# Expert blocks of 32 slots in four column groups, with conditional further blocks, one scatter for four experts and two more ring places

## The chip, the cores and the metric

The kernel runs on one core of a Trainium2 chip. The time is that of one execution on the device, in microseconds. Three executions of the kernel before gave 1189.7, 1192.71 and 1199.96 us; their median, 1192.71 us, is the figure to compare with. About 1% is what a measurement of this kernel can tell from no change.

A core has TensorE (PE; its weight loads are listed apart as PEld), VectorE (DVE), ScalarE (ACT), GpSimd (POOL) and SyncE (SP), which here issues the transfers of the weights. Every engine has an instruction stream of its own, and all five take each branch of the program by themselves.

## What is computed

One layer of a streaming encoder on 256 tokens of 1024 channels: token mixing (state space and latent attention), then 32 experts of which each token uses four. The change lies in the experts alone:

```python
logits = (h @ w_router).astype(jnp.float32) + b_router.astype(jnp.float32)
top_vals, top_idx = lax.top_k(logits, TOP_K)          # TOP_K = 4, N_EXPERTS = 32
gates = jax.nn.softmax(top_vals, axis=-1)
...
gu = xb @ w_gate_up[e] + b_gate_up[e]                 # 1024 x 2048 of each expert
glu = jnp.minimum(gu[:, :D_FF_EXPERT], SWIGLU_LIMIT)
lin = jnp.clip(gu[:, D_FF_EXPERT:], -SWIGLU_LIMIT, SWIGLU_LIMIT)
act = glu * jax.nn.sigmoid(SWIGLU_ALPHA * glu) * (lin + 1.0)
y = act @ w_down[e] + b_down[e]                       # 1024 x 1024 of each expert
return y * g[:, None].astype(y.dtype)
```

Weights and activations are float32. All 32 experts have at least three tokens, so every expert's 12 MB of weights are read once. Counted with the reference's own inputs, the experts 0 to 31 have 28, 70, 19, 8, 59, 32, 20, 24, 3, 26, 28, 53, 43, 14, 61, 29, 30, 27, 34, 51, 25, 9, 32, 35, 58, 20, 24, 37, 32, 31, 43 and 19 tokens: eleven have more than 32, and one, expert 1, more than 64.

## The kernel before

**Loads.** An expert's weights come in 12 loads of 1 MB: eight `gu` (128 rows of the first matrix) and four `dn` (256 rows of the second). `Stream` (line 72 on) keeps the list of loads in order and a list of free buffers; a load goes out on SP's queue as soon as a buffer is free, and `done` gives a buffer back. `RING` (line 69) is 7; buffers of the token mixing join the ring when they fall free, so that in the expert stage there are 18 places.

**One expert** is computed for `CAP` = 64 slots. `gather(e + 1)` (L1170) picks the next expert's tokens by a matmul with one-hots, `gathered` turns them (L1178, four transposes) and scales them into `xT`. `up` (L1191) multiplies `xT` with the first matrix: 32 matmuls of 64 weight columns and 512 streamed columns, two of which run beside each other in the two column halves of the array (the trace lists each float32 matmul as two). `up_out` copies the two banks out (`gs`, ACT L1196 and DVE L1197), `act` turns them with eight transposes (L1207) and applies bias, limits and the sigmoid on DVE and ACT. `down` (L1235) multiplies `ac` with the second matrix: 16 matmuls of 64 by 512. Each second expert, `scatter` (L1270) brings two experts' rows back to their tokens with a gated one-hot (`spread_cols`, `spread_mats` L1259) and DVE adds them to `acc` (L1271).

**Order on TensorE.** TensorE's instructions stand in the order in which the code is written. `down(e - 1)` stands in the middle of `up(e)`, so that the chain from `up` to `ac` on ACT and DVE (copy, transposes, activation) is covered by the first matmuls of the next expert.

**More than 64 tokens.** `overflow` (L1348 to L1362) reads the expert's count into a register of every engine and jumps over its body if the count is at most 64. The body takes further blocks of `OV` = 32 slots in four column groups: gather (L1292), `guo` (L1315), transposes (L1321), activation (L1326 to L1331), `pyo` (L1341), scatter. Short matmuls that nobody reads (`warm`, L1276) stand in the waits of the body. For odd experts the first block is outside of the loop. The jump stands after `up`, only for experts 0, 2, 3 and 31 after the first quarter of it. The places of an expert's `gu` loads are given back after that body (`done` in the loop over the experts).

**The end.** The last expert's second product comes in three parts (`pyl`, L1501), each followed by its scatter (`fin`, L1475), the square sums of the norm and the output.

Of the kernel before, what the change touches and what calls it, by code (L numbers as in the profile page):

```python
# [9 lines left out]
F32 = mybir.dt.float32  # L10
# [34 lines left out]
def constants():  # L45
    """Tables that depend on shapes alone, one row per partition."""
# [18 lines left out]
# rows of the tile of parameters that are turned into columns  # L65
# [41 lines left out]
def body(ctx, tc, a, out, ne=NE):  # L107
# [98 lines left out]
    def ld_nat(k0):  # L206
        """Columns of dt, q_a, k_rope, kv_a."""
# [53 lines left out]
    def ld_last(k):  # L261
        """Four slices of a half of the columns, the second half after the first and by its own halves."""
# [54 lines left out]
    def rstd_of(ss, n, width, name, r=None):  # L317
        """1 / sqrt(ss / width + eps)"""
# [7 lines left out]
    # ================================ token mixing ============================================  # L326
    with ExitStack() as fc:
# [6 lines left out]
        def two(shape, name):  # L334
            """One of two buffers in turn."""
# [14 lines left out]
        def transpose_rows(src, nk, evac_fn, tag, first=0):  # L350
            """evac_fn(k0, n, bank): src[p, t, k*128:...]^T, two k a bank."""
# [9 lines left out]
        # c -> silu, 32 equal columns for each slice of d  # L361
# [40 lines left out]
        # x normalised, transposed  # L402
# [12 lines left out]
        def split(w, th, tl_, n=2048, eng=V, parts=1, heng=A):  # L415
            """Two float32r parts that add up to w."""
# [11 lines left out]
        def mm3(o, x2_, w2, start, stop, **kw):  # L428
            """o += (x0 + x1)(w0 + w1) without x1 w1"""
# [4 lines left out]
        # shift and scale of the first norm, a quarter of d at a time: the tensor engine adds up the  # L434
        # partitions, which leaves columns
# [86 lines left out]
        # parameters by column  # L522
# [17 lines left out]
        # The tensor engine's work from here to the output projection is issued in the order in which it is written.  # L540
        # Attention and the state space run beside each other, the other modulation rows between them.
# [11 lines left out]
        # the gate of the state space  # L553
# [19 lines left out]
        def rope(dst, src, t, n, cos, sin):  # L573
            """dst, src [P, n, 32] of token tile t"""
# [35 lines left out]
        # the other modulation rows: of a group of four 512 wide, on partitions 0, 32, 64, 96  # L610
# [6 lines left out]
        def weighed(k):  # L617
            """The first of the two groups: the slices of d are added up before the tensor engine adds up the partitions."""
# [33 lines left out]
        # convolution over tokens, channels on the partitions  # L652
# [12 lines left out]
        # softplus: max(v, 0) + log1p(exp(-|v|)), log1p(e) = 2 atanh(e / (2 + e))  # L665
# [534 lines left out]
    def act(e, gs, parts=1):  # L1200
# [16 lines left out]
        for i in range(parts):  # L1217
# [6 lines left out]
            if i + 1 < parts:  # L1224
                biased(i + 1)
# [323 lines left out]
```

## Time and profile before

| what | value |
|---|---|
| three executions | 1189.7, 1192.71, 1199.96 us (median 1192.71) |
| the profiled execution | span 1197.9 us |
| TensorE busy | 1081.8 us, 90% of the span |
| DVE, ACT, POOL busy | 38%, 16%, 6% |
| bytes moved | 449.52 MB, 375 GB/s over the span |
| queue of the weights | its packets take 93.1% of 16 DMA engines' span |

The span of the profiled execution is 5.2 us over the median. The token mixing fills the first 190 us; the experts run from 192 us to 1160 us, and the end of the last expert and the output take the rest. In the views, a row of TensorE that begins with 128*64 128x512 is a matmul of 128 rows, 64 weight columns and 512 streamed columns; 128*32 has 32 weight columns. What stands in brackets or behind a bar is the idle time of the engine just before the row and what ended it. "PEq L1349" as a releaser is TensorE's own sequencer at the branch of `overflow`.

### The profile page before, as it was taken

The numbers are of one execution on the slowest core, as the hardware profiler recorded it, in microseconds if no ns is written. First come the engines' busy times: TensorE is split into PE (matmuls) and PEld (weight loads), VectorE is DVE, ScalarE is ACT, GpSimd is POOL, SyncE is SP. The second block draws the span as 40 slices with busy tenths as digits, with TensorE's granted clock in tenths as the row PEclk, the third lists the DMA queues.
The fourth block names the chain that finished last, engine by engine and source line by source line (L and its number), as shares of the span: only waits on it lengthen the run. The fifth ranks groups of instructions, "written<-read, shape, count | busy, mean of one in ns | idle before, by whom it ended". The sixth has DMA issues, their size and how long they took to land. (4 is left out here: it accounts for less than half of the span.)

```text
span 1197.9 us, 13360 instructions
## 1 busy us (share of the span) xinstructions
PE 1081.8 (90%) x5082; PEld 458.4 (38%) x5082; DVE 449.7 (38%) x921; ACT 190.5 (16%) x364; POOL 67.9 (6%) x68
## 2 busy tenths in 40 slices
PE   4999998988998999999989998979898999998887
PEld 3876673333333333333323332323332233333233
DVE  7968744333232323232323232323232133323123
ACT  5375441110000001000000000000000000000003
POOL 1265330000000000000000000000000000000000
PEclk9899998999999999999989998989998889999899
DMA  9969798689989999999999999999999999999980
GB/s 326 337 227 375 262 371 327 275 331 396 389 343 409 416 410 416 417 416 416 417 416 416 416 417 416 417 416 415 395 416 417 417 365 380 416 417 415 416 314 36
DMA packets 95982, 449.52 MB, mean 375 GB/s; under 512 B 10306, under 2 KB 23343, under 8 KB 61011
## 3 DMA queue, kind: packets, MB, share of 16 engines
q1 hardware_dynamic: 95410, 447.43, 93.1%
q8 instruction: 92, 1.51, 0.5%
q14 instruction: 64, 0.52, 0.1%
q10 hardware_dynamic: 416, 0.07, 0.0%
HBM read 446.42 MB, written 1.05 MB: 374 GB/s over the span
## 5 line engine op out<-in xcount | busy, mean ns | idle before, releaser
L1191 PE MATMUL gu<-gu,xT 128*64 128x512 f32 x2048 | 473.7, 610 | 11.7 <-DMA gu<-in_w_gate_up 8.5
L1191 PEld LDWEIGHTS gu<-gu,xT 128*64 128x64 f32 x2048 | 145.9, 140 | 291.3 <-issue 271.9
L1235 PE MATMUL py<-dn,ac 128*64 128x512 f32 x992 | 221.9, 600 | 5.7 <-DVE ac L1223 4.3
L1235 PEld LDWEIGHTS py<-dn,ac 128*64 128x64 f32 x992 | 72.7, 139 | 150.2 <-issue 133.0
L1244 DVE COPY cm<-py 64x512 f32<-64x512 f32 x30 | 20.8, 694 | 214.4 <-ACT cm L1243 214.4
L1270 PE MATMUL pc<-cm,gtm 128*128 128x512 f32 x120 | 70.3, 721 | 16.1 <-PEq L1349 9.0
L1197 DVE COPY gs<-gu 128x512 f32<-128x512 f32 x31 | 21.4, 691 | 168.1 <-PE gu L1191 168.1
L1271 DVE TENSOR_TENSOR acc<-acc,pc 128x512 f32<-128x512 f32 x68 | 46.6, 687 | 73.7 <-PE pc L1270 73.6
L1207 PE MATMUL tp<-ident,gs 128*128 128x128 f32 x256 | 39.1, 298 | 38.3 <-PEq L1349 29.6
L1196 ACT COPY gs<-gu 128x512 f32<-128x512 f32 x32 | 18.7, 585 | 318.2 <-PE gu L1191 318.2
L1170 PE MATMUL pg<-x,oh 128*64 128x512 f32 x256 | 62.7, 608 | 4.1 <-PEq L1349 3.6
L1214 DVE TENSOR_TENSOR u<-tp,biasT 128x512 f32<-128x512 f32 x64 | 42.1, 686 | 50.9 <-PE tp L1207 38.6
L1180 DVE TENSOR_TENSOR xT<-pgt,md 128x512 f32<-128x512 f32 x32 | 22.1, 692 | 90.7 <-PE pgt L1178 90.7
L1207 PEld LDWEIGHTS tp<-ident,gs 128*128 128x128 f32 x256 | 31.8, 152 | 62.5 <-issue 55.8
L1512 POOL TENSOR_TENSOR x<-x,acc 128x512 f32<-128x512 f32 x1 | 1.3, 1262 | 957.6 <-ACT acc L1511 957.6
L1243 ACT COPY cm<-py 64x512 f32<-64x512 f32 x30 | 17.4, 579 | 195.3 <-PE py L1235 195.3
L1270 PEld LDWEIGHTS pc<-cm,gtm 128*128 128x128 f32 x120 | 23.1, 221 | 62.1 <-issue 30.5
L1220 ACT ACTIVATE sg<-u 128x512 f32<-128x512 f32 (+1 forms) x33 | 20.4, 618 | 129.7 <-DVE u L1219 129.7
L1166 DVE TENSOR_SCALAR oh<-cst,rkp,r 128x64 f32<-128x64 f32 x64 | 17.1, 311 | 59.2 <-PE pg L1170 59.2
L1172 ACT COPY xg<-pg 128x512 f32<-128x512 f32 x32 | 18.7, 585 | 111.0 <-PE pg L1170 111.0
L1170 PEld LDWEIGHTS pg<-x,oh 128*64 128x64 f32 x256 | 18.8, 139 | 41.4 <-issue 40.5
L1251 DVE TENSOR_SCALAR go<-cst,rkp,gate 128x64 f32<-128x64 f32 x128 | 30.1, 308 | 0.7 <-DVEq L1349 0.6
(401 smaller groups left out, 964.2 us busy)
## 6 DMA issues: line engine op xcount, KB each, us to landing
gu<-in_w_gate_up SPq DMA_DIRECT2D x256, 1024.0 KB, 17.7
dn<-in_w_down SPq DMA_DIRECT2D x126, 1024.0 KB, 19.9
ada<-in_w_ada SPq DMA_DIRECT2D x16, 1024.0 KB, 5.0
mod<-in_w_ada SPq DMA_DIRECT2D x16, 512.0 KB, 9.5
xbc<-in_w_in SPq DMA_DIRECT2D x4, 1024.0 KB
wo<-in_w_out SPq DMA_DIRECT2D x4, 1024.0 KB
z<-in_w_in SPq DMA_DIRECT2D x2, 1024.0 KB, 5.5
nat<-in_w_in SPq DMA_DIRECT2D x4, 392.0 KB
```

The lines of the kernel that those rows point to most:

```text
L1170: T.matmul(pg[64 * h : 64 * h + 64, :], oh[:, t, :], x[:, t, h * 512 : h * 512 + 512], start=t == 0, stop=t == TT - 1)
L1180: V.tensor_tensor(xT.rearrange("p (h q) s -> p q h s", h=2), pg, a2.rearrange("p (h q) -> p q h", h=2)[:, :, :, None].to_broadcast([P, 4, ...
L1191: T.matmul(gu[h][64 * g : 64 * g + 64, :], xT[:, k, :], ws[k][:, g * 1024 + h * 512 : g * 1024 + h * 512 + 512], start=k == 0, stop=k == K ...
L1197: copy(gs[1], gu[1])
L1207: T.transpose(tp[f // 4][:, f % 4].rearrange("p g s -> p (g s)"), gs[f // 4][:, f % 4 * P : (f % 4 + 1) * P], ident)
L1214: V.tensor_tensor(u[:, hs], tp[h], bv[:, hs, :, None].to_broadcast([P, 4, 2, CAP]), op=OP.add)
L1220: A.activation(sg[:, fs], u[:, fs, 0, :], AF.Sigmoid, scale=1.702)
L1235: T.matmul(py[64 * g : 64 * g + 64, :], ac[:, f, :], wd(f, ch), start=f == 0, stop=f == FT - 1)
L1244: V.tensor_copy(comb[(e & 1) ^ 1][64:128, :], py[64:128, :])
L1251: V.tensor_scalar(go[:, t, j, :], iota, rkp[:, t, ee : ee + 1], gate[:, t, ee : ee + 1], op0=OP.is_equal, op1=OP.mult)
L1270: T.matmul(pc, lhs(t, ch), rhs(ch), start=bias is None, stop=True)
L1271: V.tensor_tensor(acc[:, t, ch * 512 : ch * 512 + 512], acc[:, t, ch * 512 : ch * 512 + 512], pc, op=OP.add)
```

## The change

- **Slots.** The first block of an expert is 32 slots instead of 64. `up` takes the four quarters of the 2048 columns into four column groups of one bank: 32 matmuls of 32 by 512, four beside each other. There is one bank to copy (`gs`, by ACT alone) and four transposes instead of eight.
- **Second product.** `down` takes four quarters of 256 columns into four column groups, turned by `e % 4`, so that four experts fill the 128 rows of two banks: 32 matmuls of 32 by 256. It stands right behind `act` of the same expert; the next expert's `up` follows it.
- **Scatter.** Once for four experts: 8 matmuls of 128 by 256 instead of 4 of 128 by 512 for each two.
- **Further blocks.** `more_up` stands ahead of every expert's `up`: if the count is over 32 it computes slots 32 to 63 from the same `xT` (up, one-hots, activation, into `ovs`), and inside of that, if the count is over 64, a loop over further blocks from a gather of their own. `more_down` stands between `act` and `down` and finishes the second block with `ov_down` (product, copy, scatter). `warm` isn't called there any more.
- **Ring.** `RING` is 9, so 20 places in the expert stage; smaller tiles and a smaller scratch size pay for it. The `gu` places are given back after each of the main `up`'s quarters, the `dn` places within `down`.

The core of the diff:

```diff
-RING = 7
+RING = 9
...
+    def up(xT, ws, s0=0, ks=range(KT), gu=None):
+        if gu is None:
+            gu = mp.tile([P, 512], F32, tag="gu", name="gu", bufs=2)
         for k in ks:
-            for h in range(2):
-                for g in range(2):
-                    T.matmul(gu[h][64 * g : 64 * g + 64, :], xT[:, k, :], ws[k][:, g * 1024 + h * 512 : g * 1024 + h * 512 + 512],
-                             start=k == 0, stop=k == KT - 1)
+            for j in range(4):
+                T.matmul(gu[OV * j : OV * j + OV, :], xT[:, k, s0 : s0 + OV], ws[k][:, j * 512 : j * 512 + 512], start=k == 0, stop=k == KT - 1)
+        return gu
...
+    def down(e, ac, wd, release):
+        i = e % 4
...
         for f in range(FT):
-            for g in range(2):
-                ch = g ^ swap
-                T.matmul(py[64 * g : 64 * g + 64, :], ac[:, f, :], wd(f, ch),
-                         start=f == 0, stop=f == FT - 1)
-        return py
+            for q in range(4):
+                o = OV * ((q + i) % 4)
+                T.matmul(group["py"][q // 2][o : o + OV, q % 2, :], ac[:, f % 4, f // 4, :], wd(f, q * 256, 256), start=f == 0, stop=f == FT - 1,
+                         skip_group_check=True)
+            release(f)
...
+    def more_up(e, n, xT, wg, wd):
+        with tc.If(n > OV):
+            with tc.If(n > CAP):
+                rk = tl([P, TT], "rk")
+                V.tensor_scalar(rk, rkp[:, :, e], float(CAP), None, op0=OP.subtract)
+                with tc.For_i(0, (n - CAP + OV - 1) // OV, 1):
+                    xo = ov_gather(rk)
+                    ov_mats(e, iota[:, :OV], lambda t: rk[:, t : t + 1])
+                    ov_act(e, up(xo, wg))
+                    ov_down(wd)
                     V.tensor_scalar(rk, rk, float(OV), None, op0=OP.subtract)
-
-            if first == CAP:
-                blocks()
-            else:
-                with tc.If(n > first):
-                    blocks()
-                V.tensor_scalar(rk, rkp[:, :, e], float(CAP), None, op0=OP.subtract)
-                ov_down(wd, ov_up(e, rk, wg, tag))
+            gu = up(xT, wg, OV)
+            ov_mats(e, iota[:, OV : 2 * OV], lambda t: rkp[:, t, e : e + 1])
+            ov_act(e, gu)
+            if e == ne - 1:
+                ov_down(wd)
+
+    def more_down(n, wd):
+        with tc.If(n > OV):
+            ov_down(wd)
...
     for e in range(ne):
         wg = [st_.take(f"gu{e}_{k}") for k in range(KT)]
-        wdp, wd = wd, weights_down(e)
-        ahead = e in (0, 2, 3, last)
...
+        wd = weights_down(e)
+        n = nc.values_load(cnt[0:1, e : e + 1], min_val=0, max_val=S)
+        more_up(e, n, xT, wg, wd)
...
+        gu = some_up(range(0, 2))
         if e < last:
             xg = gather(e + 1)
...
+        act(e, turned(gs), ub, sg, ac)
+        if e < last:
+            more_down(n, wd)
+            down(e, ac, wd, lambda f: st_.done(f"dn{e}_{f - 1}") if f % 2 else None)
+            xT = xTn
```

How this stands on TensorE, before: the piece from the last three loads of one expert's `down` (L1235) through the next expert's `up` (L1191) to the branch of `overflow` (L1348, L1349). x4 is the number of matmuls of the row.

```order
L1235 MATMUL py<-dn_2_3625,ac 64x512 x4
L1235 MATMUL py<-dn_4_3627,ac 64x512 x4
L1235 MATMUL py<-dn_6_3629,ac 64x512 x4
L1191 MATMUL gu<-gu_2_3715,xT 64x512 x4
L1191 MATMUL gu<-gu_3_3717,xT 64x512 x4
L1178 MATMUL pgt<-ident,xg 128x128 x4
L1191 MATMUL gu<-gu_4_3719,xT 64x512 x4
L1191 MATMUL gu<-gu_5_3721,xT 64x512 x4
L1191 MATMUL gu<-gu_6_4089,xT 64x512 x4
L1191 MATMUL gu<-gu_7_4091,xT 64x512 x4
L1348 TENSOR_LOAD cnt
L1349 COMPARE_AND_BRANCH
```

The same place after the change: from `more_down` (L1324, L1330) through `down` (L1222) of one expert to the two branches ahead of the next expert's `up` (L1334 is the one on 32, L1335 the one on 64).

```order
L1196 MATMUL tp<-ident,gs 128x128 x4
L1351 COMPARE_AND_BRANCH
L1324 MATMUL pyo<-dn_0_1509,ovs 32x512 x4
L1330 MATMUL pc<-yo,gb 128x512 x4
L1351 UNCONDITIONAL_BRANCH x2
L1222 MATMUL py<-dn_0_1509,ac 32x256 x8
L1222 MATMUL py<-dn_2_1587,ac 32x256 x8
L1222 MATMUL py<-dn_4_1589,ac 32x256 x8
L1222 MATMUL py<-dn_6_1591,ac 32x256 x8
L1397 TENSOR_LOAD cnt
L1334 COMPARE_AND_BRANCH
L1335 COMPARE_AND_BRANCH
```

Before, 16 matmuls of 64 by 512 stood directly ahead of the branch; now the four rows of `down` stand there, and `down` has moved from the middle of the next expert's `up` to a place right behind its own `act`. In the built program the jump over `more_up` is 436 or 437 of TensorE's instructions long for experts 0 to 30, and the one over the loop inside of it 287; before, the jump over `overflow` was 329 long for even experts and 637 for odd ones.

On DVE, after the change, the second half of one expert: the bias of its activation (L1202, into the tile called `gb`), the branch of `more_down` with its additions, and what is left of the activation.

```order
L1202 TENSOR_TENSOR gb<-tp,biasT 128x4x64 x2
L1351 COMPARE_AND_BRANCH
L1256 TENSOR_TENSOR acc<-acc,pc 128x512 x4
L1351 UNCONDITIONAL_BRANCH x2
L1203 TENSOR_SCALAR gb<-gb 128x512
L1205 TENSOR_SCALAR gb<-gb 128x4x64
L1206 TENSOR_TENSOR sg<-sg,gb 128x256
L1207 TENSOR_TENSOR ac<-sg,gb 128x256
```

Before, the activation (L1214 to L1223) stood in one piece behind the branch. Now an expert with more than 32 tokens finishes its second block on DVE between the first two operations of its activation and the rest.

## Rows read from the trace of the kernel before

**Rows 1.** The page: its first line, and the queue of the weights.
```profile
span 1197.9 us, 13360 instructions
...
q1 hardware_dynamic: 95410, 447.43, 93.1%
```

**Rows 2.** Stretches of the span; the last three columns: granted clock, DMA share, GB/s.
```profile
190.00:260.00 70.00, 64.11 (x351) 22.73 (x351) 24.05 (x64) 10.03 (x16) 0.42 (x1) 1.00 0.78 302
260.00:360.00 100.00, 95.99 (x426) 34.94 (x428) 34.33 (x68) 9.53 (x16) 0.00 (x0) 0.97 0.90 364
360.00:840.00 480.00, 436.88 (x1946) 157.05 (x1944) 148.82 (x288) 42.76 (x72) 0.00 (x0) 0.96 1.02 415
840.00:1160.00 320.00, 290.82 (x1244) 103.39 (x1242) 90.33 (x168) 27.09 (x46) 0.00 (x0) 0.93 1.00 405
1160.00:1198.00 38.00, 28.90 (x136) 12.18 (x132) 12.98 (x29) 9.29 (x24) 1.26 (x1) 0.94 0.13 45
```

**Rows 3.** TensorE's timeline over one expert: start, length (us), line, operation, [idle before].
```profile
643.65 3.65 PE L1191 MATMUL gu<-gu,xT 128*64 128x512 f32 x16
647.14 1.89 PE L1170 MATMUL pg<-x,oh 128*64 128x512 f32 x8
648.96 7.09 PE L1235 MATMUL py<-dn,ac 128*64 128x512 f32 x32
...
659.41 0.66 PE L1178 MATMUL pgt<-ident,xg 128*128 128x128 f32 x4
659.99 7.09 PE L1191 MATMUL gu<-gu,xT 128*64 128x512 f32 x32
669.30 1.06 PE L1207 MATMUL tp<-ident,gs 128*128 128x128 f32 x8 [2.22 <-PEq L1349]
671.08 5.27 PE L1191 MATMUL gu<-gu,xT 128*64 128x512 f32 x16 [0.72 <-DMA gu<-in_w_gate_up]
```

**Rows 4.** What TensorE waited for: total us, times, longest.
```profile
PE tp L1207 <- PEq L1349: 29.6, 13, 3.2
...
PE gu L1191 <- DMA gu<-in_w_gate_up: 8.5, 6, 2.5
```

**Rows 5.** The overflow block of expert 1 in TensorE's timeline.
```profile
234.10 1.45 PE L1276 MATMUL warm<-scr,onesb 128*128 128x512 bf16 x6 [0.16 <-PEq L1362]
...
238.57 0.63 PE L1310 MATMUL pgq<-ident,goo 128*128 128x128 f32 x4 [0.61 <-DVE xTo L1305]
239.13 7.07 PE L1315 MATMUL guo<-gu,xTo 128*32 128x512 f32 x64
...
246.95 0.66 PE L1321 MATMUL tpo<-ident,gso 128*128 128x128 f32 x4 [0.21 <-ACT gso L1317]
247.44 1.89 PE L1276 MATMUL warm<-scr,onesb 128*128 128x512 bf16 x8
250.33 3.64 PE L1341 MATMUL pyo<-dn,ovs 128*32 128x512 f32 x32 [1.00 <-PE warm L1276]
254.72 3.89 PE L1270 MATMUL pc<-yo,ovt 128*128 128x512 f32 x8 [0.75 <-ACT yo L1343]
258.45 0.60 PE L1207 MATMUL tp<-ident,gs 128*128 128x128 f32 x4
```

**Rows 6.** DVE's timeline: the first operation of that block's activation.
```profile
247.65 0.76 DVE L1326 TENSOR_TENSOR uo<-tpo,biasT 128x256 f32<-128x256 f32 x2 [8.76 <-PE tpo L1321]
```

**Rows 7.** The branches of `overflow`: number, then shortest, median and longest, ns.
```profile
L1349 PEldq COMPARE_BRANCH  x33: 70/5948/6875, 192.2 to 1153.1; - x33
L1349 DVEq COMPARE_BRANCH  x33: 47/56/72, 193.6 to 1145.6; - x33
```

**Rows 8.** The first and second part of the last product in TensorE's timeline.
```profile
1178.64 5.38 PE L1501 MATMUL pyl<-dn,ac 128*64 128x512 f32 x32
...
1185.87 1.95 PE L1501 MATMUL pyl<-dn,ac 128*64 128x256 f32 x16
```

**Rows 9.** Two stretches behind the wait at 669 us, columns as in rows 2.
```profile
671.00:675.00 4.00, 3.92 (x12) 1.25 (x14) 2.84 (x5) 0.63 (x1) 0.00 (x0) 0.58 1.02 414
675.00:680.00 5.00, 5.00 (x26) 1.58 (x24) 0.54 (x2) 0.58 (x1) 0.00 (x0) 1.00 1.01 421
```

More of the change, by code (lines that the diff above doesn't have):

```diff
@@ new lines, in spread_mats, with added @@
+        for c in range(2):
+            pg = mp.tile([P, 2, TT, P], F32, tag="sm", name="pgt")
+            for r in range(2):
+                j0 = (4 - 2 * c - r) % 4
+                for t in range(TT):
+                    T.transpose(pg[:, r, t, :], go[:, t, j0 : j0 + 4, :].rearrange("p j s -> p (j s)"), ident)
+            gt.append(tl([P, 2, TT, P], f"gtm{c}", ("bgr", "pv3")[c]))
+            A.copy(gt[c], pg)
+        return gt
+    def added(t, c, pc):
+        V.tensor_tensor(acc[:, t, c * 512 : c * 512 + 512], acc[:, t, c * 512 : c * 512 + 512], pc, op=OP.add)
@@ new lines, in body, with ov_mats @@
+    gb = tl([P, 2, 512], "gb", "g1b")
+    ub = gb[:, 0, :].rearrange("p (c g h s) -> p c g h s", c=4, g=2, h=2)
+    ovt = gb[:, 1, :].rearrange("p (t c s) -> p t c s", t=TT, c=2)
+    def ov_mats(e, io, rk):
+        go = tl([P, TT, 5, OV], "goo", "pt1")
+        G.memset(go, 0.0)
+        for t in range(TT):
+            for j in (0, 2, 4):
+                V.tensor_scalar(go[:, t, j, :], io, rk(t), gate[:, t, e : e + 1], op0=OP.is_equal, op1=OP.mult)
+        pg = mp.tile([P, TT, 2, P], F32, tag="sm", name="pgq")
+        for t in range(TT):
+            for ch in range(2):
+                T.transpose(pg[:, t, ch, :], go[:, t, ch : ch + 4].rearrange("p j s -> p (j s)"), ident)
+        A.copy(ovt, pg)
@@ L1289, in ov_up, with ov_act, ov_gather @@
+    def ov_act(e, gu):
+        gs = tl([P, 512], "gso", "md1")
+        A.copy(gs, gu)
+        u = tl([P, 4, 2, 2, OV], "uo", "pv0")
+        act(e, turned(gs), u, ovs, ovs)
+    def ov_gather(rk):
+        oh = tl([P, TT, OV], "oho", "early")
+        for t in range(TT):
+            V.tensor_scalar(oh[:, t, :], iota[:, :OV], rk[:, t : t + 1], r2[:, t : t + 1], op0=OP.is_equal, op1=OP.mult)
         pg = mp.tile([P, 256], F32, tag="sm", name="pgo")
@@ L1408, in body @@
     bias = None
     last = ne - 1
+    fin = {}
+    parts = ((0, 512), (512, 256), (768, 256))
     for e in range(ne):
         wg = [st_.take(f"gu{e}_{k}") for k in range(KT)]
-        wdp, wd = wd, weights_down(e)
-        ahead = e in (0, 2, 3, last)
-        if e == last - 1:
-            finish_down(e - 1, ac, wdp)
-        if e == last:
-            py = down(e - 1, ac, wdp, 0)
-            yl = tl([P, 512], "yl", "pv2")
-            A.copy(yl, py)
-        gu = halves_of_up()
-        up(gu, xT, wg, range(0, 2))
@@ L1422, in body, with some_up @@
-        if ahead:
-            overflow(e, wg, wd, f"pr{(e + ahead) % 2}")
-            for k in range(0, 2):
+        wd = weights_down(e)
+        n = nc.values_load(cnt[0:1, e : e + 1], min_val=0, max_val=S)
+        more_up(e, n, xT, wg, wd)
+        gu = None
+        def some_up(ks):
+            made = up(xT, wg, 0, ks, gu)
+            for k in ks:
                 st_.done(f"gu{e}_{k}")
+            return made
+        gu = some_up(range(0, 2))
         if e < last:
             xg = gather(e + 1)
-        if e == last:
-            scatter(lambda t, ch: gt[64 * ch : 64 * ch + 64, 0, t, :], lambda ch: yl[64 * ch : 64 * ch + 64, :])
-        elif 0 < e < last - 1:
-            finish_down(e - 1, ac, wdp)
@@ L1432, in body @@
-        up(gu, xT, wg, range(2, 4))
+        else:
+            scatter(gt, group["comb"])
+            for t in range(TT):
+                fin[t, 1] = mp.tile([P, 512], F32, tag="pc", name="fin", bufs=2)
+                T.matmul(fin[t, 1][:, 0:256], ident, acc[:, t, 512:768], start=True, stop=False)
+        gu = some_up(range(2, 4))
         if e < last:
             xTn = gathered(e + 1, xg)
-        if e % 2 == 0:
-            go = spread_cols((e, e, e + 1, e + 1) if e == last - 1 else (e, e + 1, e + 1, e))
+        if e % 4 == 2:
+            go = spread_cols([ee for ee in range(e - 2, e + 2) if ee < last])
@@ L1443, in body @@
-        up(gu, xT, wg, range(4, 8))
-        xT = xTn
-        gs = up_out(gu, "g1b", A.copy if e == last else V.tensor_copy)
-        if not ahead:
-            overflow(e, wg, wd, f"pr{(e + ahead) % 2}")
-        for k in range(2 if ahead else 0, 8):
-            st_.done(f"gu{e}_{k}")
+        gu = some_up(range(4, 8))
+        gs = tl([P, 512], "gs", "md0")
+        A.copy(gs, gu)
         if e == ne - 8:
```

213 lines of the change are left out of this document (75 added, 138 removed).

## The prediction, written before the changed kernel ran

> **What bounds the kernel now.** I read the page first, then the stretches of the span, then TensorE's timeline over single experts, its waits, and the branches. The page gives a profiled span of 1197.9 us, and the queue of the weights is busy for 93.1% of it [rows 1]. The stretches say where it isn't: 415 GB/s from 360 to 840 us, but 302, 364 and 405 GB/s in the other three stretches of the experts [rows 2]. From 190 us on the five stretches move 70 x 302 + 100 x 364 + 480 x 415 + 320 x 405 + 38 x 45 = 388,050 KB. At 415 that takes 935 us, so without a pause the loads would end at 1125 us. They end at about 1160 + 38 x 45 / 415 = 1164 us. The 39 us between are 19 from 190 to 260 us, 12 from 260 to 360 and 8 from 840 to 1160. Behind the loads come 34 us of end.
>
> TensorE is nearly as full. One expert took 27.4 us from its first `up` to the next (643.65 to 671.08) [rows 3], against 12 loads of 1.0486 MB at 415 GB/s, 30.3 us. In the whole run it waited only 8.5 us for `gu` loads, and 29.6 us at the transposes behind the branch [rows 4]. So two clocks run beside each other, loads at 30.3 us an expert and TensorE at 27 to 30, and a gain must keep both.
>
> **TensorE, an expert with at most 32 tokens.** The overflow block of expert 1 already runs in the new form, four column groups of 32, so its rows give the prices [rows 5]: `up` 7.07 us (before 14.2: 3.65 + 3.5 + 7.09 [rows 3]). Gather 1.89 and its transposes 0.66 stay [rows 3]. The copy of the one bank leaves TensorE idle as the copy ahead of `pc` does, 0.75, and four transposes are 0.66 [rows 5]. Then TensorE waits for `ac`: nothing is left to cover the activation, since `down` is next. From DVE's first operation at 247.65 [rows 6] to `pyo` at 250.33 [rows 5] it is 2.7 us at the same sizes. `down` streams the columns of `pyo` (half the width, twice the count): 3.64 [rows 5]. A scatter of 3.89 [rows 5] and eight transposes, 1.3 at the price of the four, come once in four experts: 1.3 each. Sum: 7.07 + 1.89 + 0.66 + 0.75 + 0.66 + 2.7 + 3.64 + 1.3 = 18.7 us.
>
> **The branch.** It is the largest term that the diff doesn't show. TensorE's sequencer needs 5.95 us for a branch in the median, DVE's 0.06 [rows 7]; it issues nothing meanwhile, and TensorE lives off the matmuls already queued. Before, those were `up` at 7.09 us for 32: the idle time seen is 2.22 [rows 3], so 5.95 - 2.22 = 3.7 us, some 17 matmuls, were queued. After the change the matmuls ahead of the branch are those of `down`, 64 in 3.64 us; 17 of them last 1.0 us. The idle time grows to 5.0 us. Bounds: 2.2, as now, if the queue holds more of the shorter ones; 5.95 if it holds none. I take 5.0. The branch of `more_down` jumps over some 80 instructions while the activation runs; I give it nothing, because 2.7 us of DVE cover it, and if it were as long as the others it would cost the 3.3 us that stick out.
>
> The Trainium skill ("Runtime: NRT & Kernel Launch", Instruction fetch mechanics) says that instructions arrive in blocks of 256 with sequential prefetch only, and that a taken branch to a target outside the current window of two blocks waits for a DMA fetch. It speaks against this change: jumps of 436 would leave the window almost always, and by it nearly every expert without a second block would pay 5.0, which gives the sum below. By the idle time of 2.2 alone the sum would be 53 us less on TensorE and the loads would set the end, at 1157 us. The trace agrees with it so far as the median branch takes 5.95 us.
>
> **The clock.** Behind the idle 2.22 + 0.72 us at 669 us the granted clock was 0.58 until 675 and 1.00 after [rows 9], that is, mostly the lower level; 16 matmuls took 5.27 instead of 3.65 [rows 3]. That is 1.6 us lost behind one such pause. The new expert has two pauses, 2.7 us ahead of `down` and 5.0 behind it. I charge one, 1.6; bounds 0 and 3.2. An expert without a second block: 18.7 + 5.0 + 1.6 = 25.3 us, bounds 20.9 and 27.8.
>
> **An expert with 33 to 64 tokens** adds a second `up` 7.07, four transposes 0.63, a copy 0.75 and four more transposes 0.66 [rows 5] = 9.1; then `pyo` 3.64, its copy 0.75 and its scatter 3.89 [rows 5] = 8.3. The first 0.76 us of the main activation run under that [rows 6], the rest doesn't, because it stands behind the branch on DVE. It doesn't take the long jump, but skips the loop: between 0.1 and 5.0, I take 2.5. With the pauses, 18.7 + 9.1 + 8.3 - 0.8 + 2.5 + 0.8 for half a slow stretch = 38.6 us, bounds 35.4 and 41.
>
> **Average.** Experts 2 to 30 are 19 of the first kind and 10 of the second: (19 x 25.3 + 10 x 38.6) / 29 = 29.9 us, bounds 25.9 and 32.4. So what the narrow blocks save in two thirds of the experts, the others and the branches take back, and TensorE is again level with the loads' 30.3. The longer ring lets slow and fast experts even out; that is why an average may be used.
>
> **Expert 1** now comes with a loop and a second block: first `up` at 192 us [rows 7], expert 0 18.7 plus about 1.3, so 212. The block in the loop costs what it cost before, 258.45 - 234.10 = 24.4 [rows 5]; the loop's own synchronisation isn't in the trace (the old first block stood outside of it), 0 to 10, I take 0 because the fill-in matmuls that fall away stood only in waits. Then an expert with a second block, 35.9 without jumps: 212 + 24.4 + 35.9 = 272 us.
>
> **The loads around it.** Places of expert 0 let 12 loads go out, which last until about 228. The next place falls free when expert 1's main `up` starts, at 212 + 24.4 + 9.1 = 246. So the loads stand for 18 us, and some 3 us more ahead of its `dn` places; with up to 5 us saved at 190 us by the two more places, about 22 to 28 us stand against 31 now. The 8 us late in the run go if TensorE keeps up. The loads would end at 1125 + 25 = 1150 us, or 1160 with a slow loop.
>
> **The end.** Expert 31 from the branch on: 5.0 + 1.6, `up` 7.07, scatter 3.89, copy and transposes 0.75 + 0.66 + 1.3, activation 2.7, sums into `fin` some 3: 26 us. The last product took 19.3 us from its first part (1178.64) [rows 8] to the end of the span [rows 1], of which its matmuls were 7.3; four groups take half, so 15.7.
>
> **Sum.** TensorE: 272 + 29 x 29.9 + 26 + 15.7 = 1181 us. Loads: the last one is needed by the second part, 1197.9 - 1185.87 = 12 us before the end [rows 1, 8], so 1150 + 12 = 1162 us. The later decides: 1181, 17 us under the profiled 1197.9. The profiled execution lies 5.2 us above the median of the runs; against that median I expect 1181 - 5 = 1176, and since the two clocks are level and each delays the other now and then, 1180.
>
> **The rivals.**
> - *TensorE falls behind: slower.* With a second slow stretch in each expert, the average is (19 x 26.9 + 10 x 39.4) / 29 = 31.2, 38 us over the sum: 1181 + 38 - 5 = 1214; at the upper bounds, 32.4, 1249. It begins to decide at 30.3 an expert, where the loads can no longer hide it. For it: the clock row, where less than 3 us of pause were enough. Against it: once the ring is full the loads stand now and then, and a branch can be quicker then. 1205 to 1250.
> - *The loads alone decide.* If branches stay at the idle time of 2.2 and the clock falls seldom, TensorE averages about 26 and waits for loads: 1162 - 5 = 1157, at most 1165. For it: nothing new is needed; against it: `down` is too short to cover a branch of 5.95.
> - *No change.* The loop of expert 1 has 10 us of its own and the two more ring places give nothing, as a ring of 18 kept 415 GB/s from 360 to 840 us: 1181 + 10 - 5 = 1186, up to 1196.
>
> **How the numbers follow.** Forecast, level clocks, 1168 to 1192: 0.42. TensorE behind: 0.31. Loads alone: 0.14. No change: 0.13. A measurement of this kernel can tell about 1% from no change, so faster is under 1181 and slower over 1205. Of the forecast, 0.28 lies under 1181 and 0.14 above: faster 0.28 + 0.14 = 0.42, same 0.14 + 0.13 = 0.27, slower 0.31. The range reaches from the loads' 1157 to the middle of the slower rival, 1235, which leaves out about 0.04 below and 0.12 above. The forecast's own range is 1168 to 1192.
>
> **What would show it.** In the profile after: `gu` with 32 columns 64 times in about 7 us an expert, `down` 3.6; idle time at the branch of L1334 on TensorE of 5 us for most experts with at most 32 tokens, not 2; a wait of `py` for DVE of about 2.7 us; a granted clock under 0.9 in the stretches of the experts where it is 0.93 to 1.00 now [rows 2]; a load rate near zero between 228 and 246 us. If TensorE waits for `gu` loads in most experts, the loads decide and the time is near 1160. If the load rate is under 400 GB/s after 360 us, TensorE is behind, and the time is over 1200. I am wrong about the sum if a branch costs something else than 5 us, each us of it being 19 us of the whole, or if the activation's wait is much longer than 2.7.

## The result and the profile after

The changed kernel took 1250.81 us in the median of four runs (1246.13 to 1254.49), against 1194.42 us for the kernel before, run beside it: a ratio of 1.0436 with a 95% interval of 1.0396 to 1.0477; the two medians by themselves give 1.047, which lies in it. It is slower by 56 us by the medians and by 52 us by the ratio. The forecast was 1180 us with a range up to 1235; the rival that came true is the one in which TensorE falls behind, just past the upper end of the 1205 to 1250 that stood there.

The page of the changed kernel: its first line, busy times, and the queue of the weights (89.9%, where [rows 1] had 93.1%).

```profile
span 1249.5 us, 18112 instructions
...
PE 962.0 (77%) x7159; PEld 420.1 (34%) x7159; DVE 400.2 (32%) x955; ACT 192.7 (15%) x384; POOL 71.2 (6%) x80
...
q1 hardware_dynamic: 95410, 447.43, 89.9%
```

TensorE is busy for 120 us less than before and yet the kernel is longer: it stands still more than it saves. The stretches, with the columns of [rows 2], show where the loads stop:

```profile
190.00:260.00 70.00, 54.19 (x394) 17.76 (x398) 22.21 (x68) 10.87 (x17) 0.73 (x2) 0.88 0.60 238
260.00:360.00 100.00, 72.92 (x600) 24.69 (x592) 22.86 (x58) 8.58 (x16) 0.36 (x1) 0.91 0.99 399
360.00:840.00 480.00, 366.96 (x2856) 134.20 (x2852) 114.89 (x285) 41.03 (x77) 1.83 (x5) 0.86 0.98 399
840.00:1160.00 320.00, 239.12 (x1858) 87.03 (x1858) 78.78 (x185) 26.45 (x50) 1.25 (x4) 0.89 0.96 385
1160.00:1198.00 38.00, 28.29 (x248) 10.33 (x244) 7.37 (x20) 4.23 (x8) 0.36 (x1) 0.91 1.00 394
1198.00:1250.00 52.00, 35.12 (x258) 14.98 (x246) 17.74 (x38) 10.64 (x27) 1.26 (x1) 0.93 0.14 46
```

The long middle stretch, 415 GB/s before, is at 399, and the one behind it at 385 (405 before). TensorE is busy only three quarters of the time there, and its granted clock is 0.86 and 0.89 instead of 0.96 and 0.93. The loads wait for a machine that isn't busy. What it waited for from the end of expert 1 on (total us, times, longest), to be read against [rows 4]:

```profile
PE py L1222 <- DVE ac L1207: 91.0, 28, 5.0
PE gu L1190 <- PEq L1334: 85.9, 19, 6.2
PE gu L1190 <- issue: 12.7, 3, 5.4
PE gu L1190 <- PEq L1335: 7.9, 5, 2.6
```

There are two pauses in most experts: `down` (L1222) waits for the activation, and the first matmul of `up` (L1190) for TensorE's own sequencer at the branch (L1334; L1335 is the inner one, on 64). Waits for loads are small: 0.3 us for a `gu` load and 2.7 us for a `dn` load in the same stretch. One expert with a second block (61 tokens) and the one behind it (29 tokens) in TensorE's timeline:

```profile
647.83 7.08 PE L1190 MATMUL gu<-gu,xT 128*32 128x512 f32 x64 [1.72 <-PEq L1335]
...
672.73 3.89 PE L1330 MATMUL pc<-yo,gb 128*128 128x512 f32 x8 [0.76 <-ACT yo L1326]
681.64 5.92 PE L1222 MATMUL py<-dn,ac 128*32 128x256 f32 x64 [5.02 <-DVE ac L1207]
693.77 3.26 PE L1190 MATMUL gu<-gu,xT 128*32 128x512 f32 x16 [6.20 <-PEq L1334]
696.96 1.94 PE L1170 MATMUL pg<-x,oh 128*64 128x512 f32 x8
698.83 1.92 PE L1190 MATMUL gu<-gu,xT 128*32 128x512 f32 x16
700.68 0.66 PE L1178 MATMUL pgt<-ident,xg 128*128 128x128 f32 x4
701.27 3.64 PE L1190 MATMUL gu<-gu,xT 128*32 128x512 f32 x32
705.62 0.66 PE L1196 MATMUL tp<-ident,gs 128*128 128x128 f32 x4 [0.71 <-ACTq L1351]
709.01 5.35 PE L1222 MATMUL py<-dn,ac 128*32 128x256 f32 x64 [2.73 <-DVE ac L1207]
719.00 3.64 PE L1190 MATMUL gu<-gu,xT 128*32 128x512 f32 x16 [4.64 <-PEq L1334]
```

The same 16 matmuls of `up` last 1.92 us in the middle of the expert and 3.26 to 3.64 behind the branch; `py` lasts 5.35 to 5.92 us here, and 3.66 in c_warm below, where the clock is up. The granted clock (third column from the end) was 0.62 and 0.75 in the stretches behind the two pauses of these rows:

```profile
681.00:688.00 7.00, 5.92 (x64) 2.66 (x64) 0.55 (x2) 0.00 (x0) 0.00 (x0) 0.62 0.81 305
...
693.00:700.00 7.00, 6.23 (x36) 1.59 (x40) 0.54 (x2) 0.58 (x1) 0.00 (x0) 0.75 0.92 348
```

That holds for most experts and not for all: of the experts 1 to 30, `py` lasts 3.66 us in four, behind pauses of 2.5 to 3.3 us, and 4.96 to 6.61 in the others.

### The profile page after: what moved, and what is told of

Read it like the earlier page. It is cut to its first block, busy times and chain, and to the rows that moved or that the text cites. A ratio compares the mean times of both kernels' runs of the same rounds, so it can differ in the third digit from the quotient of the medians.

```text
span 1249.5 us, 18112 instructions
## 1 busy us (share of the span) xinstructions
PE 962.0 (77%) x7159; PEld 420.1 (34%) x7159; DVE 400.2 (32%) x955; ACT 192.7 (15%) x384; POOL 71.2 (6%) x80
## 3 DMA queue, kind: packets, MB, share of 16 engines
q1 hardware_dynamic: 95410, 447.43, 89.9%
## 5 line engine op out<-in xcount | busy, mean ns | idle before, releaser
L1190 PE MATMUL gu<-gu,xT 128*32 128x512 f32 x2752 | 353.3, 649 | 115.7 <-PEq L1334 88.8
L1222 PE MATMUL py<-dn,ac 128*32 128x256 f32 x1984 | 167.7, 512 | 101.1 <-DVE ac L1207 98.4
L1190 PEld LDWEIGHTS gu<-gu,xT 128*32 128x32 f32 x2752 | 87.7, 115 | 321.6 <-issue 301.3
L1222 PEld LDWEIGHTS py<-dn,ac 128*32 128x32 f32 x1984 | 79.4, 145 | 188.3 <-DVE ac L1207 114.9
L1330 PE MATMUL pc<-yo,gb 128*128 128x512 f32 x96 | 46.7, 618 | 9.1 <-ACT yo L1326 9.1
L1324 PE MATMUL pyo<-dn,ovs 128*32 128x512 f32 x384 | 45.4, 615 | 2.7 <-DVE ovs L1207 2.7
L1202 DVE TENSOR_TENSOR uo<-tp,biasT 128x256 f32<-128x256 f32 x24 | 9.1, 419 | 97.8 <-ACT gb L1291 89.1
L1202 DVE TENSOR_TENSOR gb<-tp,biasT 128x256 f32<-128x256 f32 x64 | 24.0, 416 | 46.0 <-PE tp L1196 46.0
L1265 PE MATMUL pc<-cm,gtm 128*128 128x256 f32 x128 | 31.9, 394 | 0.0
L451 DVE SCALAR_TENSOR_TENSOR md<-mod,cact,md 128x512 f32<-128x512 f32 x28 | 29.5, 1052 | 0.9 <-DMA mod<-in_w_ada 0.2
L1330 PEld LDWEIGHTS pc<-yo,gb 128*128 128x128 f32 x96 | 15.3, 188 | 41.5 <-ACT yo L1326 20.0
```

The lines of the kernel that those rows point to most:

```text
L451: V.scalar_tensor_tensor(ac, w[:, k, :], c, ac, op0=OP.mult, op1=OP.add)
L1190: T.matmul(gu[OV * j : OV * j + OV, :], xT[:, k, s0 : s0 + OV], ws[k][:, j * 512 : j * 512 + 512], start=k == 0, stop=k == KT - 1)
L1202: V.tensor_tensor(u[:, :, g], tp[:, :, g], bv[:, :, :, None].to_broadcast([P, 4, 2, OV]), op=OP.add)
L1222: T.matmul(group["py"][q // 2][o : o + OV, q % 2, :], ac[:, f % 4, f // 4, :], wd(f, q * 256, 256), start=f == 0, stop=f == FT - 1, skip_g ...
L1265: T.matmul(pc[:, r * 256 : r * 256 + 256], gt[c][:, r, t, :], comb[c][:, r, :], start=bias is None, stop=True, skip_group_check=True)
L1324: T.matmul(py[o : o + OV, :], ovs[:, f % 4, f // 4, :], wd(f, ch * 512, 512), start=i == 0, stop=i == 3)
```

## The experiments

**Theory 1** was that TensorE is the bound because it stands at the branch and at the activation and runs slowly after both. Its rivals: a taken branch costs the same however long the jump is (A); the arithmetic of the second blocks is the cost (B); something in the new form outside of the conditional part is slow (C). Medians of runs from different chips are compared through their ratio to the kernel before, which ran beside each (1194 to 1199 us).

**a_loop1: the jump shortened.**

```diff
-            with tc.If(n > CAP):
+            if e == 1:
```

> The loop over further blocks (slots 64 on) is in the program for expert 1 alone, the only one that needs it; so the jump over more_up is 148 of TensorE's instructions long instead of 436, and the inner jump of 287 is gone. Nothing else changes. Theory 1 (TensorE is the bound, because it stands still for the branch and for the activation and runs at the lower clock after both): most jumps become short, the idle time at that branch falls from 88.8 us in 20 places to under 30, the slow stretch after it goes too, and the time falls by 60 to 90 us to 1165 to 1190, where the loads decide. Rival A (a taken branch costs the same whatever its length): 1240 to 1250. Rival B (the arithmetic of the second blocks is what costs): 1235 to 1250.

Measured: 1184.33 us, ratio 0.9886 (0.9848 to 0.9925): 66 us come back, and it is faster than the kernel before by 1.1%. Its waits in the experts, as above:

```profile
PE py L1222 <- DVE ac L1207: 93.4, 29, 5.0
PE gu L1190 <- DMA gu<-in_w_gate_up: 60.7, 56, 2.4
PE gu L1190 <- PEq L1334: 8.2, 17, 2.8
```

The wait at the branch fell from 85.9 us to 8.2 and TensorE now waits 61 us for loads, while the wait for the activation is what it was. Rival A falls: with a shorter jump most of the price goes (i_hint below leaves the length as it is). Rival B falls as the main cause, since every second block is still there. From the end of one `py` to the end of the next, the experts 2 to 30 take 29.9 us in the mean, where the changed kernel's take 32.15: 29 x 2.25 = 65 us, nearly all of what came back.

**b_noblocks: nothing conditional.**

```diff
-        more_up(e, n, xT, wg, wd)
...
-            more_down(n, wd)
```

> more_up and more_down are left out, branches and work: tokens of an expert beyond its 32nd are not computed. Theory 1: an expert takes TensorE about 22 us, loads decide from the first expert to the last, about 415 GB/s without a stop, 1150 to 1165. It bounds what everything conditional costs (85 to 100 us). Rival C (something outside of the conditional part, the new form of up and down or the scatter of four, is slow): over 1190.

Measured: 1137.03 us, ratio 0.9482. That is under what was expected; the loads run at 404 GB/s already from 190 to 260 us and at 417 after, and the granted clock is only 0.80 from 360 us on, which costs nothing there. Rival C falls. All conditional parts together cost 114 us.

**k_never: all jumps, no second block.** The same line changes in `more_up` and in `more_down`.

```diff
-        with tc.If(n > OV):
+        with tc.If(n > S - 1):
```

> The branches of more_up and more_down stay with their long jumps, but compare with 255 instead of 32, so that no expert takes a second or further block: tokens beyond the 32nd are not computed. Theory 1 as it stands after the first runs (only together do second blocks and jumps exceed the loads' 30.3 us: an expert without a second block is at 27 to 28): loads decide, 1140 to 1160, near the 1137 without any conditional part, although every expert pays the jump and the lower clock. If the jumps alone are too much: 1180 or more.

Measured: 1151.66 us, ratio 0.9607 (0.957 to 0.964). The branch of L1334 on TensorE (number, then shortest, median, longest in ns):

```profile
L1334 PEldq COMPARE_BRANCH  x32: 447/6009/6449, 190.6 to 1107.2; - x32
```

23 of the 32 branches take 5.9 to 6.5 us and TensorE waits 118 us at 26 of them, and still it costs 15 us over no conditional part, 11 of them before the end of expert 1. Jumps alone cost 15, second blocks and the loop without long jumps 47 (a_loop1 against b_noblocks), both together 114. The two don't add, because what an expert pays on TensorE is free as long as the loads are later: from expert 2 on an expert takes 29.8 us in the mean in k_never and in b_noblocks alike.

**c_warm and h_warm_act: matmuls in the pauses.** c_warm has both lines, h_warm_act only the first.

```diff
             more_down(n, wd)
+            warm(10)
             down(e, ac, wd, ...)
+            warm(17)
             xT = xTn
```

> Short matmuls that nobody reads stand in both pauses of every expert: 10 ahead of down, 17 behind it (ahead of the next branch). They can't shorten a pause, they only keep TensorE busy in it. Theory 1 with the clock as a full part of it: the granted clock of the experts' stretches rises from 0.86 to 0.89 to over 0.95, py goes from 5.4 back to 3.7 us, the first 16 matmuls of up from 3.6 to 1.9; some 3 us an expert come back, while the 17 cost about 3.7 us in the ten experts that are not preceded by a long jump: 1170 to 1215. If the clock isn't a cause: 1250 to 1290.

Measured: 1259.92 us, ratio 1.0522 (1.0456 to 1.0587), 9 us worse than the changed kernel and in the range that stood for a clock that is no cause. Its timeline behind one expert:

```profile
712.68 3.66 PE L1222 MATMUL py<-dn,ac 128*32 128x256 f32 x64
716.28 3.84 PE L1271 MATMUL warm<-scr,onesb 128*128 128x512 bf16 x16
723.70 1.92 PE L1190 MATMUL gu<-gu,xT 128*32 128x512 f32 x16 [3.58 <-PEq L1334]
```

The clock came back (0.97 from 360 to 840 us; `py` 3.66, `up` 1.92), as theory 1 said, but the fill-in ahead of the branch made the way from `py` to `up` 3.84 + 3.58 = 7.4 us (6.7 to 7.4 at the 14 longest branches) instead of 4.5 to 6.2. The traces show why. In both kernels the long branches begin when 14 to 20 matmuls are left to run. In the changed kernel these are the last of `py`, 1.0 to 1.9 us; in c_warm they are the fill-in matmuls, 3.4 us, so the branch begins 0.4 us behind the end of `py` and not ahead of it. What the clock gave, the delay took: an expert without a second block took 27.0 us (27.6 in the changed kernel), one with a second block 42.6 (40.8). So the run can't tell what the clock is worth by itself.

> The changed kernel (long jumps) with 10 short matmuls that nobody reads ahead of down only, in the pause for the activation; none ahead of the branch. Before this, with 17 more ahead of the branch, the clock rose to 0.97 but the branch began later by what they took. Theory 1: py goes from 5.4 to 3.7 us in most experts, the branch's idle time grows by 0.5 as the queue ahead of it is shorter in time, the slow stretch behind the branch stays: 28 x 1.2 = 34 us, 1210 to 1225. If the clock behind the first pause costs nothing in the end: 1245 to 1255.

Measured: 1233.55 us, ratio 1.0317 (1.0265 to 1.0369): 17 us better than the changed kernel (14 by the ratios), half of what was expected. `py` is at 3.66 us in every expert, but the waits at the branches grew:

```profile
PE gu L1190 <- PEq L1334: 100.1, 19, 6.0
PE warm L1271 <- DVE gb L1202: 29.2, 21, 2.9
PE gu L1190 <- PEq L1335: 22.8, 8, 5.4
```

With the few us that the view puts down to "issue", that is 126 us at the branches instead of 107: a slow `down` had been covering part of the branch. `py` gave back 153.1 - 102.5 = 50.6 us; 19 of them went into these waits, and some 10 into the fill-in itself, which with the waits ahead of it takes 100 us where the waits for the activation had taken 90. So taking away the lower clock behind the first pause was worth 14 to 17 us.

**d_cover and e_loop1_cover: `down` back in the middle of `up`.** The first with the long jumps, the second with a_loop1's short ones.

```diff
             xg = gather(e + 1)
+        if e:
+            down(e - 1, ac, wdp, ...)
...
             more_down(n, wd)
-            down(e, ac, wd, ...)
+            wdp = wd
```

> down of the expert before stands behind the first quarter of up and the gather, as it stood before the change; more_up and more_down stay where they are. Theory 1: the wait of py for the activation, 98 us in 30 places, falls under 10, while the branch has fewer matmuls ahead of it and stands 5 to 6 us instead of 4.4; with one pause less there is one slow stretch less: 29 x (3.2 - 1 + 1.7) = some 110 us, more than there is to the loads' limit, so 1165 to 1195. If the activation's wait only moves into the branch's wait (both end at the same time): 1215 to 1250.

Measured: 1216.34 us, ratio 1.0137 (1.0096 to 1.0178). The wait for the activation is gone, 34 us come back, and the rest moved as the other reading said: `up` now waits 99.9 us at 16 branches of L1334, up to 7.6 us, since only four transposes stand directly ahead of them.

> The short jump (loop for expert 1 alone) and down of the expert before behind the first quarter of up, together. With the short jump alone, 1184, loads go at 412 to 417 GB/s from 360 to 1100 us and TensorE already waits 61 us for them. Theory 1 (what is left there is the stop of the loads around expert 1 and the end, not TensorE's pauses): no more than 10 us come back, 1172 to 1186, although the wait for the activation (93 us) goes. If TensorE's pauses still cost on the path: 1150 to 1168.

Measured: 1190.1 us, ratio 0.9932 (0.9911 to 0.9952), no better than a_loop1's 0.9886 and outside of both ranges. From 190 to 260 us the loads move 204 GB/s instead of 242: `down(0)` now stands behind the further blocks of expert 1, so its four places come free after them. 38 x 70 KB are 2.7 MB, 6 us, which is the difference. The wait for the activation, 93 us in a_loop1, is gone from its list, and TensorE waits 160.5 us for `gu` loads instead of 60.7: the pauses of TensorE no longer matter once the jumps are short.

**f_noloop: the hold around expert 1.**

```diff
-            if e == 1:
+            if e == -1:
```

> The short jump, and the loop isn't run for expert 1 either: its tokens 65 to 70 are not computed. Only the hold around expert 1 changes, by the 23 us of one block. Theory 1: the loads stand some 23 us less from 190 to 260 us (242 GB/s with the loop), and all of it reaches the end: 1155 to 1165. If the later experts would have made that time good anyway: 1175 to 1184.

Measured: 1159.76 us, ratio 0.9686 (0.9641 to 0.9731): 24.6 us, one block of the loop, all of it at the end. Here every microsecond in which expert 1 holds its places is paid.

**g_loop1_ring7 and n_before_ring9: the ring alone.** The first is a_loop1 with `RING = 7`, the second the kernel before with `RING = 9` and the smaller scratch.

> The short jump with RING = 7, so 18 places instead of 20 in the expert stage. The prediction gave the two places up to 5 us, once, ahead of 200 us. Theory 1: 1186 to 1192 against 1184. If the longer ring is what evens out slow and fast experts: 1195 to 1210. If it is of no use: 1182 to 1186.

> The kernel before with RING = 9 and the smaller scratch alone (64 slots, jumps and overflow as before). The two places give up to 5 us ahead of 200 us and let loads run on in the late stretch, where 8 us of stops were: 1183 to 1194 against 1194 to 1198. If the ring's length isn't what holds the loads: no change.

Measured: 1188.69 us, ratio 0.9921 (0.9890 to 0.9952), 4 us over a_loop1 with intervals that overlap; and 1202.81 us, ratio 1.0039 (1.0021 to 1.0056), no gain, where 1183 to 1194 were expected. The two places are worth a few us at best, and nothing where TensorE is behind.

**i_hint: the jump's target named ahead.**

```diff
-        with tc.If(n > OV):
+        with tc.If(n > OV, label=f"more{e}"):
...
             more_down(n, wd)
+            tc.mark_branch_hint_location(f"more{e + 1}", "LikelyTaken", engines=[mybir.EngineType.PE])
```

> The changed kernel with all its long jumps, and on TensorE one instruction more for each expert that names the target of the next expert's jump over more_up some 290 instructions ahead of it, so that the target can be fetched beforehand. Theory 1 (the idle time at the jump is the fetch of its target): the median of that branch falls well under 1 us, the idle time from 88.8 us to under 30, and the time to 1180 to 1200, as with the short jump (1184). If the instruction comes too early or isn't heeded: 1245 to 1256.

Measured: 1197.94 us, ratio 1.0000 (0.9978 to 1.0021): the 52 us that the change had cost by the ratios are gone with one instruction for each expert, all long jumps and the general loop still there. Where the changed kernel had 16 jumps of 5.8 to 7.1 us among the 21 that are taken, one is left over 5 us (5.20), four are between 3.3 and 5.0, and most are 0.33 to 0.47. The branch on TensorE (the median of the changed kernel, 314 ns, is no measure here, as the experts that don't jump are in it):

```profile
L1334 PEldq COMPARE_BRANCH  x43: 79/331/5204, 193.6 to 1158.6; - x43
```

The wait at L1334 is 14.2 us instead of 85.9; the one at the inner branch, whose target isn't named, is 32.9. This is the sharpest test of rival A: the same branches, over jumps as long as before, at a twentieth of the time.

The trace of the changed kernel also shows the fetch itself. Into each of its 18 branches of L1334 that last over 3 us falls one packet of 16 KB on the queue of the instructions (q8 of the page); it takes 0.9 to 1.2 us, and the branch ends 1.4 to 1.6 us after it has landed. Into none of the 24 branches under 1 us falls such a packet.

**l_before_e1, m_before_e1_ring9, o_before_hint_ring9: the same cures on the kernel before.** l keeps the branch of `overflow` for expert 1 alone; m is l with `RING = 9`; o is the kernel before with `RING = 9`, every branch in place and the instruction of i_hint. Its edit:

```diff
-        with tc.If(n > CAP):
+        with tc.If(n > CAP, label=f"ov{e}"):
...
         ahead = e in (0, 2, 3, last)
+        tc.mark_branch_hint_location(f"ov{e}", "LikelyTaken", engines=[mybir.EngineType.PE])
```

> The kernel before with RING = 9, and overflow's branch and loop in the program for expert 1 alone, so no jump in the other experts. Nothing is left out of the computation with these inputs. TensorE loses the 30 to 40 us in which it stood behind the branch; an expert takes it 26 to 27 us, so loads go at 415 GB/s from 260 to 1160 us and only the stop at expert 1 and the end are left: 1165 to 1182. If the branch cost the kernel before nothing because the loads decided anyway: within 3 us of the ring's run.

> The kernel before (RING = 7) with overflow's branch and loop in the program for expert 1 alone. With RING = 9 as well it took 1164 us, with RING = 9 alone no less than before. Theory 1 (the long jump is what held TensorE, and through it the loads, in the kernel before too): 1164 to 1172. If only the two together give it (the ring needs TensorE free, TensorE needs the ring): 1180 to 1192.

> The kernel before with RING = 9, its overflow for every expert and every count, and one instruction more for each expert on TensorE that names the jump's target ahead of it. In the changed kernel that instruction took 52 us of the 56 away. Theory 1: the median branch falls from 5.95 us to under 0.5, and the time from 1199 to 1165 to 1180, with nothing specialised to the counts. If the jump's fetch isn't what holds the kernel before: 1190 to 1203.

Measured: m 1163.99 us, ratio 0.9697 (0.9655 to 0.9740); l 1169.67, ratio 0.9762 (0.9713 to 0.9810); o 1181.67, ratio 0.9859 (0.9812 to 0.9906). The stretches of l from 260 to 1100 us:

```profile
260.00:360.00 100.00, 99.80 (x462) 35.41 (x460) 34.70 (x69) 10.12 (x17) 0.00 (x0) 1.00 1.00 409
360.00:840.00 480.00, 441.05 (x1980) 158.37 (x1978) 153.25 (x295) 44.02 (x74) 0.00 (x0) 0.96 1.02 417
840.00:1100.00 260.00, 241.15 (x1046) 82.60 (x1044) 75.68 (x145) 22.36 (x38) 0.00 (x0) 0.94 1.02 418
```

Without jumps the loads run at 409 to 418 GB/s from 260 us on where [rows 2] show 364 to 415. And the branch of `overflow` in o, against [rows 7]:

```profile
L1349 PEldq COMPARE_BRANCH  x33: 83/336/4414, 198.1 to 1137.9; - x33
```

The median branch fell from 5.95 us to 0.34. So the idle time of some 2 us at the branch held the kernel before as well. o differs from n_before_ring9 by the instruction alone: 1.0039 against 0.9859, some 22 us. It came out just over the 1165 to 1180 that were expected. o computes everything for any counts and is faster than both kernels; m is the fastest run of those that leave nothing out with these inputs, with a branch for the one expert that needs it. Why o stays 18 us over m wasn't tried: its inner branches and loops are still in the program, and it has 380 GB/s from 260 to 360 us where m has 401.

## Why the prediction was wrong

**What bounds the kernel: right.** Loads at 30.3 us an expert and TensorE close under it; the later one decides. After the change an expert took 32.15 us, where a_loop1, k_never and b_noblocks, in which the loads decide, took 29.8 to 29.9. So TensorE was the later one by 2 us an expert, and that is nearly the whole result.

**The branch: right, and decisive.** The prediction put the idle time at 5.0 us; it was 85.9 / 19 = 4.5 in the mean of the experts without a second block, and 4.5 to 6.2 in 16 of them. It came from the shape of what is queued ahead: 17 matmuls lasting 1.0 us were put; in the trace 14 to 20 are left when a long branch begins, lasting 1.0 to 1.9 us, and h_warm_act and c_warm confirm that reading.

**The clock: the step that failed.** The prediction saw that one pause of 2.9 us had cost 1.6 us [rows 3, 9] and that the new expert has two pauses, and charged one. Both cost: in the mean of the 19 experts without a second block `py` lasts 5.56 instead of 3.66 us and the first 16 matmuls of `up` 3.32 instead of 1.92, 3.3 us instead of 1.6. An expert without a second block took 27.6 us, where 25.3 stood in the sum. (From the end of one `py` to the end of the next, 19 experts; the first and the last of the 30 rows from expert 1 on are these.)

```profile
278.13 3.66 PE L1222 MATMUL py<-dn,ac 128*32 128x256 f32 x64 [3.33 <-DVE ac L1207]
...
1209.10 5.04 PE L1222 MATMUL py<-dn,ac 128*32 128x256 f32 x64 [3.85 <-DVE ac L1207]
```

**The second block: 40.8 us instead of 38.6.** The wait for the activation behind `more_down` was 2.5 to 5.0 us, 3.5 in the mean of the ten experts, where 1.9 was put (2.7 less the 0.8 done ahead). At the expert with 61 tokens nothing was done ahead: DVE made the four additions of the second block, then one-hots for the scatter, and only then the whole activation. These are its rows (start, length):

```profile
676.66 0.69 DVE L1256 TENSOR_TENSOR acc<-acc,pc 128x512 f32<-128x512 f32 x1 [0.17 <-PE pc L1330]
677.26 1.53 DVE L1238 TENSOR_SCALAR go<-cst,rkp,gate 128x32 f32<-128x32 f32 x7
678.71 0.74 DVE L1202 TENSOR_TENSOR gb<-tp,biasT 128x256 f32<-128x256 f32 x2
```

A slow `py` comes on top, 5.25 us in the mean.

**Expert 1: 282 us instead of 272.** Expert 0 met both pauses and a slow `py` too, the loop's block took from 219.84 to 246.93, 27.1 instead of 24.4, and the first `up` began 4 us later than before. (By its own terms the 35.9 in that sum is 35.3, and the 192 us read from [rows 7] are the first branch's; `up` began at 191.5. Neither moves the 272 by more than 1 us.)

**The end: 35 us instead of 42** from the last `down` on; `pyl` to the end of the span is 1249.5 - 1233.7 = 15.8, as worked out (15.7).

**The sum, term by term.** Expert 1 gave +10, the 29 experts 29 x (32.15 - 29.9) = +65, the end -6: 1181 + 69 = 1250. The error sits in 2.2 us for each of 29 experts. Of the 65 us, 19 x (3.3 - 1.6) = 32 are the clock in the experts without a second block, and 10 x (1.6 + 0.8) = 24 are the wait and the slow `py` of those with one. That is how the sum was missed; it isn't what a cure of the clock gives back, since h_warm_act got 14 to 17 us.

**The rivals.** "TensorE falls behind" named the second slow stretch and gave 31.2 to 32.4 us an expert; measured were 32.15. It was given 0.31. (The forecast's upper bound, 1235, was called the middle of 1205 to 1250, which is 1228.) The reason to hold it down, that a branch could be quicker when the ring is full, didn't show: the branches of the changed kernel mostly took 5.8 to 7.1 us. "The loads alone decide" is what happens without long jumps, but then at 1184, not 1157. The loads of a_loop1 ended at about 1154 us, near the 1150 that were put; but that is 28 us ahead of the end of the span and not 12, as the last `up` and the last product still stood behind them.

**The Trainium skill** ("Runtime: NRT & Kernel Launch", Instruction fetch mechanics), by which a taken branch waits for a DMA fetch if its target is outside of the current window, was weighed as speaking against the change, and the traces agree: 18 of the 21 jumps taken over `more_up` took 3.6 to 7.1 us, each with one packet of instructions in it, and a_loop1, i_hint and o_before_hint_ring9 show that the target's fetch, and not the branch, is the cost, 6 us when it isn't there and 0.2 to 0.4 when it is.

**What was read too lightly** is that the kernel before paid the same fetch. The prediction listed 39 us of stops in its loads and put most of them to expert 1; l_before_e1, in which the branch and its body are in the program for expert 1 alone, is 28 us under the kernel before, and naming the target took 22 us off in o, a price that [rows 4] show as 29.6 us of waits at one place alone. Compared without long jumps and with the same ring, the narrow blocks lose even then: 0.976 against 0.992 with `RING` at 7 (l_before_e1, g_loop1_ring7), 0.970 against 0.989 with 9 (m_before_e1_ring9, a_loop1), 19 and 23 us. About half of that is the longer hold of expert 1, whose second block now also runs ahead of the `up` that gives its places back. From 190 to 260 us the loads of m_before_e1_ring9 and of a_loop1 moved 310 and 242 GB/s, first m_before_e1_ring9:

```profile
190.00:260.00 70.00, 64.26 (x352) 22.55 (x355) 21.66 (x63) 10.04 (x16) 0.42 (x1) 0.98 0.80 310
```

and a_loop1:

```profile
190.00:260.00 70.00, 55.14 (x408) 17.64 (x410) 22.82 (x68) 10.93 (x17) 0.73 (x2) 0.90 0.62 242
```

That is 68 x 70 KB = 4.8 MB, 11 of the 23 us; f_noloop showed that such time isn't made good later. Where the other half lies no run shows.

## What to carry to other kernels

Before work is moved ahead of a branch, ask how long the queue ahead of the branch lasts in time, not in instructions: faster matmuls there laid the fetch of the jump's target bare. Where a jump skips hundreds of instructions, name its target ahead of time or make the skipped code short; in the changed kernel either was worth 52 us and more, and the next best thing that was tried and left nothing out, `down` back in the middle of `up`, 34. When two clocks are level, a term of 2 us for each of 30 experts is the whole answer, so charge every pause with what the trace shows behind one such pause.

## What the runs showed of the hardware

A jump over 436 instructions took TensorE's sequencer 5.8 to 7.1 us in 16 of 21 cases (6.0 in the median of k_never), one over 148 mostly 0.2 to 0.4; DVE's branches at the same line took 0.05, in an instruction stream of its own whose length wasn't varied. In each long one the trace has one instruction packet of 16 KB. Naming the target some 290 instructions ahead brought most of the long ones to 0.33 to 0.47 us. The long branches of the changed kernel and of c_warm began when 14 to 20 matmuls were left to run, so it is their time that covers a branch: 4.0 us in most of those of the kernel before, 1.0 to 1.9 in the changed kernel. With 16 short ones more behind `py`, taking 3.84 us, the way from one expert's `py` to the next `up` was 7.4 us where it had been 4.5 to 6.2. And the granted clock of 0.80 in b_noblocks from 360 us on cost nothing, because the loads decided there.
